# The gate products of a decoder trunk: two column tiles per call or four, on four accumulation banks

## The chip, the cores and the metric

The kernel runs on one core of one Trainium2 chip. The metric is the device time of one execution in microseconds (us); the figure given for a kernel is the median of its runs. One execution was also recorded by the hardware profiler, and the views of the profile come from that execution. In those views PE is TensorE's matrix multiplication, PEld its loading of the stationary operand, DVE is VectorE, ACT is ScalarE, POOL is GpSimd and SP is SyncE, which issues most of the DMA transfers. L253 means line 253 of the kernel that the view belongs to.

## The reference

Two layers of a post-norm decoder trunk, 256 tokens of width 1024, all in float32. Each layer is

```
x <- LN(alpha*x + 0.5*SwiGLU_1(x))
x <- LN(alpha*x + Mixer(x))
x <- LN(alpha*x + 0.5*SwiGLU_2(x))
```

with a feed-forward width of 2816. The change lies in the mixer:

```
z = x @ w_in                       # -> u | v | q | k | val | gate_A | gate_B, 1024 columns each
u, v = gelu(u), gelu(v)
h_a = u * chunked_causal_mix(LN(v))                      # branch A
q, k = rope(q), rope(k)                                  # 8 heads, 2 x 64
o = softmax(q1 k1^T) val - lam * softmax(q2 k2^T) val    # branch B, causal
h_b = rmsnorm(o) * (1 - lam_init)
m = sigmoid(gate_A) * (h_a @ W_A) + sigmoid(gate_B) * (h_b @ W_B)
Mixer(x) = m @ w_out
```

## The kernel before

**Numbers.** TensorE works on float32 values rounded to a shorter form (float32r). Each operand v is held as two parts, hi = v rounded and lo = v - hi, and a product is taken as hi*hi + lo*hi + hi*lo. The activations of a layer are kept as such pairs in `x_cat`: for each slab k of 128 of the 1024 inputs, 512 columns, of which the first 256 are the hi part of the 256 tokens and the last 256 their lo part. `both(k)` is that 512-column slab.

**Weights.** `stream` (L156 to L172) brings 1 MB of weights by one DMA from SP's queue into a buffer `raw` (four of them). ACT rounds it into `whi` (L169) and DVE subtracts into `wlo` (L171), each in two pieces of 128x1024, a piece being one column tile of 128 outputs with its eight slabs of inputs. There are eight buffers for hi pieces and eight for lo pieces. The order of TensorE's instructions is the order in which the program writes them; that of the other engines is set by a scheduler when the program is built, from priorities (`step()` raises them with every weight transfer) and from explicit orders (`behind(...)` places an instruction after a named one). Each engine runs its own queue in order.

**The products with outputs on the partitions, `gemm_a2`.** A call takes a list of sources of 1 MB, each two column tiles. For every tile it takes a bank and issues eight matmuls of 512 columns with `whi` as the stationary operand (L253): the bank's left half gets hi*hi, the right half hi*lo. When all the call's tiles have had this wide pass, each gets a narrow one: eight matmuls of 256 columns with `wlo` onto the left half (L260). Behind a tile's narrow pass ACT copies the right half to `r` (L261), and DVE adds the left half to it (L263, or L265 where there is a scale). The result, two tiles to a buffer of 512 columns, is called `gz` in the gates, `z` in the queries and keys, `bz` in the branch products; `r` and these are of a pool of three buffers in the gates.

**Banks.** PSUM has eight banks, in two rings of four. `bank()` gives out the main ring, in turn: a call of one source takes two main banks, a call of two sources all four. `side_bank()` gives the side ring, used by attention, transposes and the position mixing. A bank can be written again once both of its readers, ACT's copy and DVE's add, are done.

**Order of the mixer.** First `val`; then, for each of four pairs of heads, a call for the queries and one for the keys, each with its rotation in `rope`: two DMAs on SP's queue swap the rows (L601), DVE multiplies by the cosines (L604), POOL the swapped rows by the sines (L605), and DVE sums the two (L609). Then gate A in four calls of one source, gate B in four, `u` in two, the `v` products, `u` in two more, and the branch products, which use calls of two sources. Behind each gate call ACT takes two tanh (L735), one for each tile.

**Attention beside the products.** What attention needs is cut into steps that are placed between the tiles of the running products by a clock: each tile's wide pass counts 0.65 and each narrow pass 0.35 (`beat`), and a step is issued when its delay has run out. For one pair of heads the steps are: scores on TensorE (L629) with the row maxima on DVE (L641) and eight exponentials on ACT (L643); the combination of the two softmaxes on DVE (L652, behind a reciprocal at L660 and L661); a rearrangement by POOL (L184), a transposing DMA on SP's queue (L188), and four copies on ACT (L677); the product with the values on TensorE (L683, L685); its copy and its squares on ACT (L688, L693); a reciprocal root on POOL; four scalings on ACT (L702); and a second transposition with two roundings. The pairs start `4.5 + 2.1 * hp` counts after their keys, so the four pairs' steps are spread over the gate calls and the calls behind them.

Of the kernel before, what the change touches and what calls it, by code (L numbers as in the profile page):

```python
# [16 lines left out]
AF = mybir.ActivationFunctionType  # L17
# [5 lines left out]
T = 256  # L23
NT = T // P
KT = D // P
# [28 lines left out]
def trunk(ctx, tc, x, xT, w13a, w13b, w2, wb, wqk, wa, wbr, wo, gateb, sgug, sgub, sguwT, sgubias, lam, diffg,  # L54
          lng, lnb, lngT, lnbT, cosT, sinT, out):
    nc = tc.nc
    V, A, G, PE = nc.vector, nc.scalar, nc.gpsimd, nc.tensor
# [15 lines left out]
    def name(s):  # L73
        serial[0] += 1
        return f"{s}_{serial[0]}"

    def bank():
        return psum.tile([P, 512], F32, tag="main", name=name("bank"))

    def side_bank():  # L80
        return psum.tile([P, 512], F32, tag="side", name=name("sbank"))

    def slots(s, n, dtype=F32):

        return [act.tile([P, 512], dtype, tag="slot", name=name(s)) for _ in range((n + 1) // 2)]
# [11 lines left out]
    def t512(s, n=3):  # L97
        return tmp.tile([P, 512], F32, tag="main", name=name(s), bufs=n)

    def s512(s, n=4):  # L100
        return tmp.tile([P, 512], F32, tag="side", name=name(s), bufs=n)
# [21 lines left out]
    def beat(w):  # L123

        clock[0] += w
        for task in list(tasks):
            if task[0] <= clock[0]:
                turn(task)
# [21 lines left out]
    def stream(src, width=CH, sub=HC, lent=(), after=(None, None)):  # L150

        step()
        raw = raw_pool.tile([P, CH], F32, tag="raw", name=name("raw"))
        loaded[0] = nc.sync.dma_start(raw[:, :width], src).ins  # L156
        out = []
        for o in range(0, width, HC):
            if o // HC in lent:
                hi, lo = ([act.tile([P, 512], F32R, tag="slot", name=name(n)) for _ in range(2)] for n in ("lhi", "llo"))  # L160
                at = [(hi[j], lo[j]) for j in range(2)]
            else:
                hi = hi_pool.tile([P, HC], F32R, tag="hi", name=name("whi"))
                lo = lo_pool.tile([P, HC], F32R, tag="lo", name=name("wlo"))
                at = [(hi[:, p : p + sub], lo[:, p : p + sub]) for p in range(0, HC, sub)]
            for p, (h, w) in zip(range(0, HC, sub), at):
                r = raw[:, o + p : o + p + sub]
                with behind(latest[0]):
                    A.activation(h, r, AF.Copy)  # L169
                with behind(after[o // HC] or latest[1]):  # L170
                    V.tensor_tensor(out=w, in0=r, in1=h.bitcast(F32), op=ALU.subtract)  # L171
            out.append((hi, lo))  # L172
        return out
# [69 lines left out]
    def gemm_a2(srcs, xc, zs, rs=lambda: s512("r"), scale=1.0):  # L243

        b, got = [], []
        for src in srcs:
            got += stream(src)
            for hi, _ in got[-2:]:  # L250
                b.append(bank())
                for k in range(KT):
                    PE.matmul(b[-1], hi[:, k * P : (k + 1) * P], xc(k), start=k == 0, stop=False)  # L253
                beat(0.65)
        for n, (_, lo) in enumerate(got):
            s = slice(n % 2 * T, (n % 2 + 1) * T)
            if n % 2 == 0:
                r, z = rs(), zs(n // 2)
            for k in range(KT):
                PE.matmul(b[n][:, :T], lo[:, k * P : (k + 1) * P], xc(k)[:, :T], start=False, stop=k == KT - 1)  # L260
            emptied[0] = A.activation(r[:, s], b[n][:, T:], AF.Copy, scale=scale).ins  # L261
            if scale == 1.0:
                a = V.tensor_tensor(out=z[:, s], in0=b[n][:, :T], in1=r[:, s], op=ALU.add)  # L263
            else:
                a = V.scalar_tensor_tensor(out=z[:, s], in0=b[n][:, :T], scalar=scale, in1=r[:, s], op0=ALU.mult,  # L265
                                           op1=ALU.add)
            added[0] = a.ins
            beat(0.35)
            if n % 2:
                yield n // 2, z  # L270
# [95 lines left out]
    b = side_bank()  # L366
# [11 lines left out]
    gbh = const.tile([P, DEPTH, 2, KT], F32, name="gbh")  # L378
# [202 lines left out]
    def mixer(l, i, norm):  # L581
# [146 lines left out]
        for br, sec in ((0, GA_), (1, GB_)):  # L728
            gt = slots("gate", KT)
            gates.append(gt)  # L730
            for c in range(KT // 2):
                (_, b), = gemm_a2([wa[l, sec, c]], both, lambda m: t512("gz"), lambda: t512("r"))
                for n in range(2):
                    s = slice(n * T, (n + 1) * T)
                    A.activation(gt[c][:, s], b[:, s], AF.Tanh, scale=0.5,  # L735
                                 bias=gbh[:, l, br, c * 2 + n : c * 2 + n + 1])

        g_bc, b_bc = (bc_load(v[l], gates[0][0][:, :1]) for v in (sgug, sgub))
        us = []
# [30 lines left out]
        for h in range(2):  # L770
            s = slice(h * 512, h * 512 + 512)
# [57 lines left out]
    for l in range(DEPTH):  # L829
        norm = ffn(l, 0, 0, norm)  # L830
        norm = mixer(l, 1, norm)
        norm = ffn(l, 1, 2, norm, last=l == DEPTH - 1)
# [83 lines left out]
```

## Time and profile before

| | |
|---|---|
| median of three runs | 1220.29 us |
| the three runs | 1219.65, 1220.29 and 1221.74 us |
| the profiled execution | 1220.37 us |
| its span, first to last instruction | 1218.6 us |
| matmuls and weight loads | 6079 each |
| instructions of DVE, ACT, POOL | 1516, 1372, 392 |
| HBM read, written | 235.47 MB, 1.05 MB, together 194 GB/s over the span |
| granted TensorE clock | 9 of 9 tenths in every slice |

The span is what the profiler recorded between the first and the last instruction. In the page of the profile the busy time of an engine stands with its share of the span and, behind the x, its number of instructions. The chain is found from the last instruction backwards: at each step it goes to what released that instruction, or to the one before it on its engine, so its shares say which engine held the end. A row of the timeline gives start, duration, engine, line, operation, output and input, and, where the engine had been idle before it, that idle time with what ended it in brackets. `x2` there is two instructions, in one row; the duration then is of both.

### The profile page before, as it was taken

Reading aid. Unit: us, or ns where it says so; the run is one execution under the profiler, and the core shown is the slowest. Engines: PE = TensorE matmul, PEld = TensorE weight load, DVE = VectorE, ACT = ScalarE, POOL = GpSimd, SP = SyncE. Lnnn points to the kernel's source line nnn. Section 1 sums busy time; section 2 is a strip of 40 time slices with the busy share of each in tenths; the row PEclk is TensorE's granted clock in tenths of the full one; section 3 lists DMA queues with packets and bytes.
Section 4 is the critical chain, followed back from the end, with each engine's and each line's share of the span. In section 5 each row is a group of like instructions: output and inputs, shape, how many; then the busy total and the mean of one; then the engine's idle time right before and its main releaser. Section 6 shows DMA issues by size and latency. Waiting matters only on the chain.

```text
span 1218.6 us, 17027 instructions
## 1 busy us (share of the span) xinstructions
PE 1212.8 (100%) x6079; PEld 1025.6 (84%) x6079; DVE 887.9 (73%) x1516; ACT 716.0 (59%) x1372; POOL 283.1 (23%) x392
## 2 busy tenths in 40 slices
PE   9999999999999999999999999999999999999998
PEld 8888888888888888888888888888888888888887
DVE  6676667897688986766676756678875989676763
ACT  6465546669865555554455554466797664564740
POOL 1523100155320023230023330003544000323200
PEclk9999999999999999999999999999999999999999
DMA  9967645659564746867556757556675746667540
GB/s 343 328 196 240 242 173 178 242 192 274 194 214 144 250 157 211 246 203 259 190 164 204 250 194 259 205 183 221 215 206 189 250 155 226 189 224 243 178 185 35
DMA packets 103653, 257.55 MB, mean 211 GB/s; under 512 B 68320, under 2 KB 69392, under 8 KB 77456
## 3 DMA queue, kind: packets, MB, share of 16 engines
q1 hardware_dynamic: 99600, 243.82, 59.2%
q0 software_dynamic: 3536, 12.13, 3.3%
q8 instruction: 47, 0.77, 0.2%
q10 hardware_dynamic: 432, 0.52, 0.1%
q14 instruction: 38, 0.31, 0.1%
HBM read 235.47 MB, written 1.05 MB: 194 GB/s over the span
## 4 chain that ended last, share of the span: by engine, by line
PE 99%; DMA 0%; DVE 0%; ACT 0%; issue 0%; ACTq 0%
PE bank L241 64%; PE bank L253 19%; PE bank L260 10%; PE bank L356 2%; PE sbank L629 1%; PE sbank L507 1%; PE sbank L685 1%; PE sbank L786 1%; DMA xraw<-in_xT 0%; PE sbank L683 0%; PE sbank L479 0%; DVE xtok L487 0%; ACT whi L206 0%; DVE st L452 0%; DVE xtok L448 0%; ACT x L206 0%
## 5 line engine op out<-in xcount | busy, mean ns | idle before, releaser
L171 DVE TENSOR_TENSOR wlo<-raw,whi 128x512 fp32r<-128x512 f32 (+1 forms) x570 | 524.1, 954 | 133.1 <-ACT whi L169 87.7
L169 ACT ACTIVATE whi<-raw 128x512 fp32r<-128x512 f32 (+1 forms) x570 | 432.7, 799 | 234.3 <-PE bank L241 158.3
L241 PE MATMUL bank<-whi,x 128*128 128x512 f32 x1352 | 421.8, 390 | 0.0
L241 PEld LDWEIGHTS bank<-whi,x 128*128 128x128 f32 x1352 | 253.9, 188 | 52.6
L241 PE MATMUL bank<-wlo,x 128*128 128x512 f32 x676 | 263.1, 389 | 0.0
L253 PE MATMUL bank<-x,whi 128*128 128x512 f32 x768 | 183.9, 391 | 0.0
L253 PEld LDWEIGHTS bank<-x,whi 128*128 128x128 f32 x768 | 141.5, 188 | 28.1
L184 POOL COPY planes<-planes 128x512 uint16<-128x512 uint16 x80 | 83.3, 1068 | 321.2 <-DVE planes L539 321.2
L241 PEld LDWEIGHTS bank<-wlo,x 128*128 128x128 f32 x676 | 127.0, 188 | 25.7
L241 PE MATMUL bank<-whi,hhi 128*128 128x512 f32 (+1 forms) x374 | 141.2, 378 | 0.0
L241 PE MATMUL bank<-wlo,hhi 128*128 128x512 f32 (+1 forms) x374 | 141.0, 377 | 0.0
L241 PE MATMUL bank<-whi,hlo 128*128 128x512 f32 (+1 forms) x374 | 140.8, 377 | 0.0
L260 PEld LDWEIGHTS bank<-x,wlo 128*128 128x128 f32 x768 | 97.9, 191 | 3.6
L260 PE MATMUL bank<-x,wlo 128*128 128x256 f32 x768 | 100.4, 284 | 0.0
L192 POOL COPY planes<-planes 128x512 uint16<-128x512 uint16 x80 | 70.5, 925 | 91.7 <-DMA planes<-planes 91.4
L539 DVE TENSOR_TENSOR planes<-planes,bank 128x512 f32<-128x512 f32 x40 | 27.3, 683 | 86.4 <-issue 70.8
L538 ACT ACTIVATE planes<-bank 128x512 f32<-128x512 f32 x40 | 24.0, 599 | 102.8 <-PE bank L241 101.8
L605 POOL TENSOR_TENSOR swap<-swap,sin_t 128x512 f32<-128x512 f32 x16 | 29.5, 1843 | 235.0 <-DMA swap<-z 202.6
L241 PEld LDWEIGHTS bank<-whi,hlo 128*128 128x128 f32 x374 | 70.4, 188 | 13.1
L241 PEld LDWEIGHTS bank<-whi,hhi 128*128 128x128 f32 x374 | 70.4, 188 | 12.8
L241 PEld LDWEIGHTS bank<-wlo,hhi 128*128 128x128 f32 x374 | 70.4, 188 | 12.5
L261 ACT ACTIVATE r<-bank 128x256 f32<-128x256 f32 x128 | 46.5, 372 | 25.6 <-PE bank L260 25.6
(179 smaller groups left out, 1288.2 us busy)
## 6 DMA issues: line engine op xcount, KB each, us to landing
raw<-in_w13b SPq DMA_DIRECT2D x76, 1024.0 KB, 5.4
raw<-in_w SPq DMA_DIRECT2D x40, 1024.0 KB, 6.0
raw<-in_wa SPq DMA_DIRECT2D x24, 1024.0 KB, 5.1
raw<-in_wb SPq DMA_DIRECT2D x16, 1024.0 KB, 5.0
raw<-in_wqk SPq DMA_DIRECT2D x16, 1024.0 KB, 4.8
raw<-in_wbr SPq DMA_DIRECT2D x16, 1024.0 KB, 5.0
raw<-in_w13a SPq DMA_DIRECT2D x8, 1024.0 KB, 5.1
raw<-in_wo SPq DMA_DIRECT2D x8, 1024.0 KB, 4.9
```

The costliest lines, as they stand in the source:

```text
L169: A.activation(h, r, AF.Copy)
L171: V.tensor_tensor(out=w, in0=r, in1=h.bitcast(F32), op=ALU.subtract)
L184: G.tensor_copy(out=planes(out)[:, w], in_=numbers(src)[:, w])
L192: eng.tensor_copy(out=numbers(out)[:, w], in_=planes(src)[:, w])
L241: PE.matmul(ps, xx, w, start=start and n == 0, stop=stop and n == 2)
L253: PE.matmul(b[-1], hi[:, k * P : (k + 1) * P], xc(k), start=k == 0, stop=False)
L260: PE.matmul(b[n][:, :T], lo[:, k * P : (k + 1) * P], xc(k)[:, :T], start=False, stop=k == KT - 1)
L261: emptied[0] = A.activation(r[:, s], b[n][:, T:], AF.Copy, scale=scale).ins
L356: PE.matmul(ps[t][m], x[:, j, o + t * P : o + (t + 1) * P], y, start=k0 + j == 0 and o == 0 and y is hi, stop=k0 + j == KT - 1 and y is lo)
L538: silu[0] = A.activation(s, ps[0], AF.Silu).ins
L539: added[0] = V.tensor_tensor(out=s, in0=s, in1=ps[1], op=ALU.mult).ins
L605: turned_by[0] = G.tensor_tensor(out=s3, in0=s3, in1=s, op=ALU.mult).ins
```

## The change

The loops over gate calls go two sources at a time. Before, each of the four calls of a gate took one source of two column tiles: two wide passes, two narrow ones. Now each of two calls takes two sources: four wide passes, then four narrow ones. It holds for both gates, in both layers: 16 calls become eight. The number and shapes of the matmuls, the weights' transfers, the copies, the adds and the tanh are the same. The counts of `beat` are the same in sum, but a wide pass counts 0.65 and a narrow one 0.35, so the attention steps fall at other places among the passes. `gemm_a2` itself is as before.

```diff
@@ -728,12 +728,13 @@
         for br, sec in ((0, GA_), (1, GB_)):
             gt = slots("gate", KT)
             gates.append(gt)
-            for c in range(KT // 2):
-                (_, b), = gemm_a2([wa[l, sec, c]], both, lambda m: t512("gz"), lambda: t512("r"))
-                for n in range(2):
-                    s = slice(n * T, (n + 1) * T)
-                    A.activation(gt[c][:, s], b[:, s], AF.Tanh, scale=0.5,
-                                 bias=gbh[:, l, br, c * 2 + n : c * 2 + n + 1])
+            for c0 in range(0, KT // 2, 2):
+                for m, b in gemm_a2([wa[l, sec, c0 + m] for m in range(2)], both, lambda m: t512("gz"),
+                                    lambda: t512("r")):
+                    for n in range(2):
+                        s, c = slice(n * T, (n + 1) * T), c0 + m
+                        A.activation(gt[c][:, s], b[:, s], AF.Tanh, scale=0.5,
+                                     bias=gbh[:, l, br, c * 2 + n : c * 2 + n + 1])
 
         g_bc, b_bc = (bc_load(v[l], gates[0][0][:, :1]) for v in (sgug, sgub))
```

Line numbers below this place are one higher in the kernel after.

## The prediction

> **What bounds the kernel now.** I read the page first (busy shares, then the chain that ended last), then the chain row by row through the gates of layer 0, then the windows and the timelines of ACT, DVE and POOL there.
>
> ```profile
> span 1218.6 us, 17027 instructions
> PE 1212.8 (100%) x6079; PEld 1025.6 (84%) x6079; DVE 887.9 (73%) x1516; ACT 716.0 (59%) x1372; POOL 283.1 (23%) x392
> PE 99%; DMA 0%; DVE 0%; ACT 0%; issue 0%; ACTq 0%
> ```
>
> The end is set by TensorE alone: 99% of the chain is PE, and no other engine holds more than a trace of it. So a faster ACT or DVE is worth nothing, and the change can only gain by making PE's own sequence shorter, or lose by making PE wait. The chain through the gates, as start, length, what (us):
>
> ```profile
> 220.59 3.65 PE bank L253 x16
> 224.24 1.91 PE bank L260 x16
> 226.16 3.65 PE bank L253 x16
> ...
> 257.45 3.65 PE bank L253 x16
> 261.11 1.91 PE bank L260 x16
> ...
> 267.63 0.22 PE sbank L683 x2
> ...
> 268.97 0.95 PE bank L260 x8
> 269.92 3.65 PE bank L253 x16
> 273.57 1.70 PE sbank L629 x15
> 275.28 2.10 PE bank L260 x16
> ...
> 293.50 1.51 PE sbank L629 x16
> 295.01 2.11 PE bank L260 x16
> ```
>
> L253 is the w_hi pass (two tiles of eight matmuls at 512 columns), L260 the w_lo pass, L629 the attention scores, L683 with L685 the product of probabilities and values. The rows abut: PE waits for nobody in the gates. The first gate call starts at 257.45, and a pair of tiles takes 5.57 (220.59 to 226.16). Scores cost 1.51 and make the pass behind them 0.2 longer, so 1.7; the value product takes 1.34 (267.63 to 268.97).
>
> What stands close behind PE there is ACT. One window, with busy time of each engine:
>
> ```profile
> 261.00:306.00 45.00, 45.00 (x281) 39.54 (x280) 36.26 (x90) 42.51 (x115) 25.33 (x48) 1.00 0.75 223
> ```
>
> The fourth busy figure is ACT: 42.51 of 45 us, against 59% over the span. It converts the weights (L169), copies the banks out (L261), does the gates' tanh, and the exponentials and scalings of attention. The clock is 1.00.
>
> **What the change removes.** PE's instructions stay the same in number and shape. Eight of sixteen changes from wide to narrow passes go. What such a change costs is seen in the branch products, which are already done four tiles at a time (whole chain, later in layer 0):
>
> ```profile
> 392.61 7.28 PE bank L253 x32
> 399.89 3.83 PE bank L260 x32
> 403.72 17.71 PE bank L241 x78
> ```
>
> Four tiles take 11.11 there, against 2 x 5.57 = 11.14: 0.03 saved per merged call, 8 calls (4 in each of 2 layers): 0.24 us, bounds 0 and 0.5. The narrow matmuls keep their pace: 3.83/32 is 120 ns, as is 1.91/16. The Trainium skill, page "TensorE: Matmul & The Clock Gate", section "LDWEIGHTS (loading the stationary operand)", gives a load as its columns over 1.2, about 107 ns here, as long as a narrow matmul streams; by it, as an estimate, twice as many narrow matmuls in a row could leave the loads uncovered. The rows just compared say they don't.
>
> **What it takes away from the cover.** There are four main banks. Until now a call used two, and the next call's w_hi went to the other two: a bank had a whole call, over 5 us, to be copied and added out. Now a call fills all four, and the next one begins on the first of them. After its last w_lo matmul the first bank has three w_lo passes, 3 x 0.96 = 2.9 us, before PE wants it again; each later bank has 0.87 more (1.83 for the w_hi tile in between, less 0.96). Draining is ACT's copy r, then DVE's add (gz), both queued in order behind whatever the built program has put there. I walk it in layer 0 by the order of the built program. ACT rows:
>
> ```profile
> 260.32 0.36 ACT L261 ACTIVATE r<-bank 128x256 f32<-128x256 f32 x1
> ...
> 261.89 2.00 ACT L169 ACTIVATE whi<-raw 128x1024 fp32r<-128x1024 f32 x2
> 263.79 0.37 ACT L261 ACTIVATE r<-bank 128x256 f32<-128x256 f32 x1
> 264.05 1.41 ACT L677 ACTIVATE aT<-d 128x512 uint16<-128x512 uint16 x2
> 265.32 0.81 ACT L677 ACTIVATE d<-d 128x256 uint16<-128x256 uint16 x2
> 265.99 0.35 ACT L261 ACTIVATE r<-bank 128x256 f32<-128x256 f32 x1
> 267.24 0.51 ACT L735 ACTIVATE gate<-gz,gbh 128x256 f32<-128x256 f32 x1 [0.89 <-DVE gz L263]
> ...
> 295.12 0.50 ACT L643 ACTIVATE pp<-pp,mx 128x256 f32<-128x256 f32 x1
> ...
> 298.64 0.63 ACT L261 ACTIVATE r<-bank 128x256 f32<-128x256 f32 x2
> 299.17 1.27 ACT L702 ACTIVATE on<-on,nwy 128x128 f32<-128x128 f32 x4
> ...
> 312.71 0.57 ACT L688 ACTIVATE on<-sbank 128x512 f32<-128x512 f32 x1
> 313.32 0.26 ACT L693 ACTIVATE sbank<-sbank 128x128 f32<-128x128 f32 x1
> ```
>
> and DVE rows:
>
> ```profile
> 260.71 0.42 DVE L263 TENSOR_TENSOR z<-bank,r 128x256 f32<-128x256 f32 x1 [0.94 <-ACT r L261]
> ...
> 281.29 0.17 DVE L660 RECIPROCAL rc<-sums 128x4 f32<-128x4 f32 x1
> 281.50 0.22 DVE L661 SCALAR_TENSOR_TENSOR c<-rc,neg_lam,sums 128x4 f32<-128x4 f32 x1
> 281.75 1.41 DVE L652 SCALAR_TENSOR_TENSOR d<-pp,c,pp 128x256 f32<-128x256 f32 x4
> ...
> 296.82 2.35 DVE L171 TENSOR_TENSOR wlo<-raw,whi 128x1024 fp32r<-128x1024 f32 x2
> 299.10 0.41 DVE L263 TENSOR_TENSOR gz<-bank,r 128x256 f32<-128x256 f32 x1
> ```
>
> Occupancy per piece, row start to row start: a conversion 0.95, r 0.27, four L677 1.94, the eight exponentials 295.12 to 298.64 = 3.52, four L702 1.2, a tanh about 0.41, L688 0.6, an L693 about 0.41 (0.26 and its readout).
>
> *First call, third tile.* It takes the bank of the last key tile, whose add ends at 260.71 + 0.42 = 261.13; PE wants it at 257.45 + 3.65 = 261.10. Wait 0.1 (0 to 0.25 with the hand-over).
>
> *PE without waits.* Call 1 with its value product ends at 269.92, as now. Call 2 has scores behind its second tile, from 273.57 as now, and ends at 273.57 + 1.7 + 3.65 + 3.83 = 282.8. Call 3 (gate B): three w_hi tiles 5.5, value product 1.34, w_hi 1.83, first w_lo 0.96, scores 1.7, three w_lo 2.9: 297.0. Call 4's second w_hi tile is wanted at 298.8, and needs call 3's second bank drained.
>
> *ACT and DVE.* Call 2's exponentials start 1.62 after the scores (293.50 to 295.12 now) and end at 275.2 + 3.52 = 278.7. DVE then needs 1.9 (281.29 to 283.16 now) for the probabilities, 1.2 for a w_lo and 0.4 for the add: 282.2. There ACT's tanh can start, and from it on ACT is never free: two tanh 0.8, r 0.27, L677 1.94, r 0.27, L702 1.2, two tanh and three conversions 3.7, L688 0.6, four L693 1.65, a conversion 0.95: 11.4, so 293.6 for the copy of call 3's first bank, which PE finished at 292.4. Copy, add and tanh: 295.0. Now eight exponentials stand ahead of the second bank's copy: 298.5, copied at 298.9; DVE's two w_lo (2.3, behind eight row maxima of 2.2 from 294.5) end at 299.05, its add at 299.45. PE waits 0.65. That is the low bound but for luck, since no hand-over and no stretched DVE row is in it. Some eight hand-overs of 0.03 to 0.1 and three w_lo stretched by 0.2 (POOL beside, below) make 1.65 the high one. I take 1.1.
>
> Covered at nothing: the temporaries (r and gz share three buffers; the next call comes 11 us later), the tanh, and the weight supply (223 GB/s in the window; the same transfers as now, conversions of two calls ahead). If that prefetch ran dry, a call's four tiles would want 2 MB in 7.3 us, 0.27 MB/us; then PE would wait on conversions.
>
> **One more wait moved.** In the built program DVE's sum of the last key tile (L609) now stands ahead of the first gate add, not behind it, and it waits for POOL's product:
>
> ```profile
> 237.87 1.29 POOL L605 TENSOR_TENSOR swap<-swap,sin_t 128x512 f32<-128x512 f32 x1 [5.75 <-DVE mx L641]
> 265.08 2.94 POOL L605 TENSOR_TENSOR swap<-swap,sin_t 128x512 f32<-128x512 f32 x1 [4.15 <-DMA swap<-z]
> 268.05 1.07 DVE L609 TENSOR_TENSOR qk<-qk,swap 128x512 f32<-128x512 f32 x1 [0.85 <-POOL swap L605]
> ```
>
> If the sum still starts at 268.05, then sum 1.0, w_lo 1.2 and add 0.4 end at 270.65, and call 2, due at 269.92, waits 0.7. But the product's 2.94 was spent beside a busy DVE; with DVE idle it may take 1.29 and the wait is 0. The Trainium skill, page "SBUF — State Buffer", section "Who interferes with whom", says that a DVE instruction with two SBUF inputs contends with a GpSimd instruction that reads SBUF; the two POOL rows agree, and by that rule the wait would be nearer 0. I take 0.2.
>
> **The sum.** Per layer 0.1 + 1.1 + 0.2 = 1.4, twice 2.8, less 0.24: +2.55. The profiled execution took 1220.37 (span 1218.6 and 1.8 around it), 0.08 over the median of 1220.29. That gives 1222.9.
>
> **Rivals.** *Drained in time (not slower).* If call 3's second add ends by 298.8, 0.65 sooner than I sum, the wait vanishes; it decides at that point, and ACT has idle time upstream (0.89 in the tanh row) to win it from. Then only 0.24 is saved: 1220.1. Against it: ACT's 11.4 us without a gap. *The sum on POOL (slower still).* L609 holds the queue the full 0.7 and the attention stretch runs late behind it, with the bank wait at 1.65: 2 x (0.25 + 0.7 + 1.65) - 0.24 = +5.0, 1225.4. *It changes nothing in PE's order* is excluded: the built program has four w_hi tiles, then four w_lo. *The bank rule.* The Trainium skill, page "Trainium Kernel Development and Optimization", section "Best Practices", warns of PSUM pressure and that regular bubbles can mean PSUM ran out; no bubble shows now, and the forecast is such a bubble.
>
> **How the numbers follow.** A change under 0.2% (2.4 us) can't be told from none: the three runs spread 2.1 us. Forecast case 0.56, its range 1221.3 to 1224.3, 0.36 of it over the bound; drained in time 0.18, split 0.17 same and 0.01 faster; POOL 0.20, slower; the rest 0.06, most of it an unseen gain, 0.05. Slower 0.56, same 0.38, faster 0.06. Range 1220.0 to 1225.8.
>
> **What would show it.** In the profile after, a gap of about 1 us in PE ahead of the second w_hi tile of gate B's second call in each layer, released by DVE's gz, with exponentials ahead of that copy on ACT; a four-tile call at 11.11. Wrong, if the gates' rows abut as now, or if PE waits on w_hi.

## The result, and the profile after

The kernel after takes 1223.60 us (median of ten runs, 1223.18 to 1224.48), the kernel before 1220.32 (ten runs beside them, 1219.65 to 1221.74). The ratio is 1.0029, with a 95% interval of 1.0020 to 1.0037: slower by 3.28 us. The prediction said 1222.9, 1220.0 to 1225.8.

The page of the profile after: its span, the busy time of the engines, and the shares of the chain that ended last.

```profile
span 1221.6 us, 17009 instructions
PE 1213.7 (99%) x6079; PEld 1025.3 (84%) x6079; DVE 887.4 (73%) x1516; ACT 716.6 (59%) x1372; POOL 277.8 (23%) x392
PE 93%; ACT 4%; POOL 1%; DVE 1%; issue 1%; DMA 0%; ACTq 0%
```

TensorE does as many matmuls as before, but the chain no longer runs on it alone: 4% lie on ACT, which had 0%. The span is 3.0 longer. The list of waits says what TensorE waited for (us in total, times, longest); before it had no row for the gates.

```profile
PE bank L253 <- DVE gz L263: 2.0, 4, 0.7
```

Four waits of the wide pass for a gate's add, two in each layer. Where they are, and what they cost, is read from the timeline of TensorE, before and then after. What stands in brackets is the idle time. It is less than the delay, since the recorded matmuls overlap (256.92 + 7.66 is later than the next start, 264.42), so delays are taken from start to start: eight wide matmuls take 1.82 (the 3.65 of sixteen, halved), 32 wide 7.28, 32 narrow 3.83.

```profile
257.29 3.82 PE L253 MATMUL bank<-x,whi 128*128 128x512 f32 x16
...
308.09 2.00 PE L253 MATMUL bank<-x,whi 128*128 128x512 f32 x8
```

```profile
256.92 7.66 PE L253 MATMUL bank<-x,whi 128*128 128x512 f32 x32
264.42 4.00 PE L260 MATMUL bank<-x,wlo 128*128 128x256 f32 x32
...
296.70 2.00 PE L253 MATMUL bank<-x,whi 128*128 128x512 f32 x8
298.97 5.78 PE L253 MATMUL bank<-x,whi 128*128 128x512 f32 x24 [0.27 <-DVE gz L263]
304.58 3.99 PE L260 MATMUL bank<-x,wlo 128*128 128x256 f32 x32
309.27 2.11 PE L253 MATMUL bank<-x,whi 128*128 128x512 f32 x8 [0.70 <-DVE gz L263]
```

Call the stretch from gate A's first matmul to `u`'s first "the stretch". In layer 0 it is 308.09 - 257.29 = 50.80 before and 309.27 - 256.92 = 52.35 after; in layer 1, read in the same way, 50.64 and 52.37. The two differences make 1.55 + 1.73 = 3.28, which is the loss within its interval (2.4 to 4.5 us); that it meets the difference of the medians to the last digit is chance. (Where only one stretch is given below, it is that of layer 0.) In layer 0 TensorE is late at three places:
- gate A's first call, third tile: 264.42 - 256.92 = 7.50, so 0.22 late
- gate B's second call, second tile: 304.58 - 296.70 = 7.88, so 0.60 late
- `u`'s first call, first tile: 309.27 - 304.58 = 4.69, so 0.86 late; this is no gate call, but it begins on the first bank that gate B's second call used.

The three make 1.68; in layer 1, read in the same way, they are 0.23, 0.56 and 0.90, so 1.69. Against the differences of the stretches that leaves -0.13 and +0.04 for all the rest: the saved changes of pass, and the scores, which take 1.60 for 1.71 in layer 0 and 1.62 for 1.54 in layer 1. A gain of 0.12 a layer can't be read out of that.

The second of them on ACT and DVE after:

```profile
294.54 0.49 ACT L643 ACTIVATE pp<-pp,mx 128x256 f32<-128x256 f32 x1
...
298.06 0.90 ACT L261 ACTIVATE r<-bank 128x256 f32<-128x256 f32 x3
300.44 0.70 ACT L702 ACTIVATE on<-on,nwy 128x128 f32<-128x128 f32 x2 [1.49 <-POOL nwy L234]
...
304.77 1.03 ACT L169 ACTIVATE whi<-raw 128x1024 fp32r<-128x1024 f32 x1
305.71 0.89 ACT L717 ACTIVATE hb<-onT,dgs 128x256 fp32r<-128x256 f32 x2
306.51 1.99 ACT L169 ACTIVATE whi<-raw 128x1024 fp32r<-128x1024 f32 x2
308.40 0.36 ACT L261 ACTIVATE r<-bank 128x256 f32<-128x256 f32 x1
```

```profile
260.19 0.41 DVE L263 TENSOR_TENSOR z<-bank,r 128x256 f32<-128x256 f32 x1
...
266.35 1.07 DVE L609 TENSOR_TENSOR qk<-qk,swap 128x512 f32<-128x512 f32 x1 [1.20 <-POOL swap L605]
...
296.23 2.36 DVE L171 TENSOR_TENSOR wlo<-raw,whi 128x1024 fp32r<-128x1024 f32 x2
298.50 0.41 DVE L263 TENSOR_TENSOR gz<-bank,r 128x256 f32<-128x256 f32 x1
...
308.80 0.42 DVE L263 TENSOR_TENSOR gz<-bank,r 128x256 f32<-128x256 f32 x1 [0.54 <-ACT r L261]
```

Eight exponentials (294.54 to 298.06) stand between the copies of gate B's first call's first and second bank; the second copy is at 298.06 and its add ends at 298.91, 0.06 ahead of TensorE's restart. Then the third place: TensorE finished the first bank of gate B's second call at about 305.54 (304.58 plus a quarter of 3.83), but ACT copies it at 308.40, and the add ends at 309.22. Ahead of the copy stand three weight conversions and two roundings for attention, none of which TensorE needs in the next 10 us: the conversions are for the `v` products, two calls ahead, whose first matmul is at 321.87, and the roundings for the branch products behind them. ACT had also sat idle for 1.49 before that, waiting for POOL's reciprocal root (300.44).

### The profile page after: what moved, and what is told of

Read it like the earlier page. It is cut to its first block, busy times and chain, and to the rows that moved or that the text cites. A ratio compares the mean times of both kernels' runs of the same rounds, so it can differ in the third digit from the quotient of the medians.

```text
span 1221.6 us, 17009 instructions
## 1 busy us (share of the span) xinstructions
PE 1213.7 (99%) x6079; PEld 1025.3 (84%) x6079; DVE 887.4 (73%) x1516; ACT 716.6 (59%) x1372; POOL 277.8 (23%) x392
## 4 chain that ended last, share of the span: by engine, by line
PE 93%; ACT 4%; POOL 1%; DVE 1%; issue 1%; DMA 0%; ACTq 0%
PE bank L241 64%; PE bank L253 16%; PE bank L260 8%; PE bank L356 2%; ACT whi L169 1%; PE sbank L507 1%; ACT gate L736 1%; PE sbank L787 1%; ACT pp L643 1%; PE sbank L629 0%; ACT sbank L693 0%; PE sbank L685 0%; ACT aT L677 0%; ACT on L702 0%; DMA xraw<-in_xT 0%
## 5 line engine op out<-in xcount | busy, mean ns | idle before, releaser
L605 POOL TENSOR_TENSOR swap<-swap,sin_t 128x512 f32<-128x512 f32 x16 | 26.8, 1676 | 234.9 <-DMA swap<-z 203.8
```

The lines of the kernel that those rows point to most:

```text
L605: turned_by[0] = G.tensor_tensor(out=s3, in0=s3, in1=s, op=ALU.mult).ins
```

## The experiments

All kept the matmuls' number and shapes; all but the first two and the last also kept the order of the kernel that they edit. Each time stands beside the kernel before on the same chip: 1220.09 for the first four, 1220.30 for the last four. Profiled executions differ by up to 2.3 us in what lies ahead of the gates, so the stretch is compared, not the span.

**Gate A alone, gate B alone.** The edit, `br == 0` in the one and `br == 1` in the other:

```diff
-            for c0 in range(0, KT // 2, 2):
-                for m, b in gemm_a2([wa[l, sec, c0 + m] for m in range(2)], ...
+            per = 2 if br == 0 else 1
+            for c0 in range(0, KT // 2, per):
+                for m, b in gemm_a2([wa[l, sec, c0 + m] for m in range(per)], ...
```

> Gate A in calls of two sources, gate B in calls of one as before. Theory (banks: the loss is TensorE waiting for main banks to be drained, at three places in each layer: gate A's first call, third tile, 0.2 us; gate B's second call, second tile, 0.55; u's first call, first tile, 0.88): only the 0.2 is left, the stretch from gate A's first matmul to u's first is 51.0 us in layer 0 (50.8 before, 52.35 with both gates changed), and the time is 0.4 over before, 1220.7. Rival (a call of four tiles costs by itself, whichever gate): half of the loss, the stretch 51.6, the time 1221.9.

> Gate B in calls of two sources, gate A in calls of one as before. Theory (banks): the waits of 0.55 at gate B's second call and 0.88 at u's first call stay, the stretch is 52.1 to 52.2 us, the time 2.8 over before, 1223.1. Rival (a call of four tiles costs by itself): half of the loss, the stretch 51.6, the time 1221.9.

Gate A alone: 1220.53, ratio 1.0002 (0.9993 to 1.0011), stretch 50.97. Gate B alone: 1223.04, ratio 1.0026 (1.0016 to 1.0035), stretch 52.07. The timeline of TensorE with gate B alone:

```profile
296.70 2.00 PE L253 MATMUL bank<-x,whi 128*128 128x512 f32 x8
299.32 5.73 PE L253 MATMUL bank<-x,whi 128*128 128x512 f32 x24 [0.62 <-DVE gz L263]
304.89 3.99 PE L260 MATMUL bank<-x,wlo 128*128 128x256 f32 x32
309.32 2.14 PE L253 MATMUL bank<-x,whi 128*128 128x512 f32 x8 [0.43 <-DVE gz L263]
```

Both waits of gate B are there, a little differently shared out (304.89 - 296.70 = 8.19, 0.91 late; 309.32 - 304.89 = 4.43, 0.60 late). So the loss is not half and half. Four tiles per call cost gate A next to nothing, with the same passes on the same four banks; they cost gate B what is ahead of its copies.

**The drain first.** The gates' copies and adds get an earlier priority (`soon`), nothing else. In the diff below, `ahead` runs its argument inside `first()`, which is `soon` for the gates' calls and does nothing for all other calls.

```diff
-            emptied[0] = A.activation(r[:, s], b[n][:, T:], AF.Copy, scale=scale).ins
+            emptied[0] = ahead(lambda: A.activation(r[:, s], b[n][:, T:], AF.Copy, scale=scale)).ins
...
-                a = V.tensor_tensor(out=z[:, s], in0=b[n][:, :T], in1=r[:, s], op=ALU.add)
+                a = ahead(lambda: V.tensor_tensor(out=z[:, s], in0=b[n][:, :T], in1=r[:, s], op=ALU.add))
...
-                                    lambda: t512("r")):
+                                    lambda: t512("r"), first=soon):
```

> The change, with the gates' copies and adds given an earlier priority: on ACT the copy of gate B's first call's second bank goes ahead of four of the eight exponentials, on DVE its add ahead of one conversion. Matmuls and their order are the same. Theory (banks): the copy comes 1.5 us and the add 1.1 us sooner, the wait of 0.55 at gate B's second call goes; the wait at u's first call stays, 0.3 to 0.9, since nothing moves ahead of the weight conversions there. The stretch is 51.5 to 51.8 us, the time about 1222.4. Rival (a call of four tiles, or the attention steps' new places among the passes, cost by themselves): as with the change, 52.35 us and 1223.6.

1221.38, ratio 1.0013 (1.0004 to 1.0022); stretch 51.17. ACT, DVE and TensorE in its timeline:

```profile
296.49 0.36 ACT L261 ACTIVATE r<-bank 128x256 f32<-128x256 f32 x1
...
299.57 0.70 ACT L702 ACTIVATE on<-on,nwy 128x128 f32<-128x128 f32 x2 [0.25 <-POOL nwy L234]
...
307.12 0.36 ACT L261 ACTIVATE r<-bank 128x256 f32<-128x256 f32 x1
```

```profile
297.34 0.41 DVE L263 TENSOR_TENSOR gz<-bank,r 128x256 f32<-128x256 f32 x1
```

```profile
296.68 7.44 PE L253 MATMUL bank<-x,whi 128*128 128x512 f32 x32
303.96 3.99 PE L260 MATMUL bank<-x,wlo 128*128 128x256 f32 x32
308.09 2.11 PE L253 MATMUL bank<-x,whi 128*128 128x512 f32 x8
```

The second bank's copy comes at 296.49 instead of 298.06, its add at 297.34 instead of 298.50, and the 32 wide matmuls take 303.96 - 296.68 = 7.28: the wait is gone. The wait at `u` fell as well, to 308.09 - 303.96 - 3.83 = 0.30, the low end of what I had given, and the stretch came out 0.33 under my range. ACT's copy there comes 1.28 earlier (307.12 for 308.40): its first scaling behind POOL's reciprocal root starts 0.87 sooner (299.57 for 300.44), and a tanh that stood behind that scaling now stands ahead of it, so that ACT is idle for 0.25 where it was for 1.49.

**The conversions of `v` behind.** They are placed after gate B's last copy and add: `stream` places its conversions behind the two instructions that `latest` holds, ACT's behind the first and DVE's behind the second.

```diff
-        us = []
+        us, latest_ends = [], (emptied[0], added[0])
...
-        u_part((0, 1))
+        u_part((0, 1)); latest[:] = latest_ends
```

> The change, with the weight conversions of the v products (ACT and DVE) placed behind the last copy and add of gate B. Matmuls and their order are the same. Theory (banks): at u's first call the copy of gate B's second call's first bank no longer stands behind three conversions, the wait of 0.88 goes to 0.1 or less; the 0.55 stays. The stretch is 51.5 us, the time about 1221.8. Rival 1 (ACT is late there because it waited 1.49 us for POOL's reciprocal root): the copy is still late and 0.5 or more of the 0.88 stays, stretch 52.0. Rival 2 (the cost is of the call itself): 52.35 us and 1223.6.

1221.29, ratio 1.0010 (1.0001 to 1.0019); stretch 51.47. ACT and TensorE:

```profile
300.55 0.69 ACT L702 ACTIVATE on<-on,nwy 128x128 f32<-128x128 f32 x2 [1.49 <-POOL nwy L234]
...
305.88 0.39 ACT L261 ACTIVATE r<-bank 128x256 f32<-128x256 f32 x1
```

```profile
299.08 5.76 PE L253 MATMUL bank<-x,whi 128*128 128x512 f32 x24 [0.27 <-DVE gz L263]
304.67 4.00 PE L260 MATMUL bank<-x,wlo 128*128 128x256 f32 x32
308.50 2.00 PE L253 MATMUL bank<-x,whi 128*128 128x512 f32 x8
```

308.50 - 304.67 = 3.83: the wait at `u` is gone, and the one at gate B's second tile stays, as expected. ACT waited just as long for POOL as with the change (1.49), so that wait alone does not make the copy late (rival 1 falls): it takes the conversions on top of it. The run before shows the other half: with the conversions in place and ACT idle for only 0.25, 0.30 of the wait was left.

**Both edits**, on the change and on the kernel before.

> The change with both edits: the gates' copies and adds earlier, and the v products' conversions behind gate B's last copy and add. Theory (banks): the waits at gate B's second call (0.55) and at u's first call (0.88) are both gone, only the 0.2 of gate A's first call is left. From the run with the first edit alone (51.18, of which 0.4 at u's first call) the stretch should be 50.8 us, as before the change; the time 1220.2. Rival (ACT and DVE have too much to do in this stretch, so that a wait taken away comes back elsewhere): 51.2 or more, 1221.2.

> The kernel before (two tiles per call) with the same two edits as both_fixed. Theory (banks): TensorE waits for nobody in the gates there, so the edits have nothing to take away: the stretch stays 50.8 and 50.6 us in the two layers, the time 1220.1. Rival (the edits help by themselves, whatever the size of a call): the time 1 us or more under before.

On the change: 1220.50, ratio 1.0003 (0.9994 to 1.0011), stretch 50.94. On the kernel before: 1219.66, ratio 0.9996 (0.9987 to 1.0004), stretch 50.68. The chain with both edits on the change:

```profile
299.09 7.28 PE bank L253 x32
306.37 3.83 PE bank L260 x32
310.20 1.84 PE bank L253 x8
```

Both came out near what I had given. The rows of gate B's second call abut again: 7.28, 3.83, then `u`. In the two stretches 0.61 of the 3.28 is left (0.14 and 0.47), about what the wait at gate A's third tile makes: that pass takes 7.53 in layer 0 and 7.72 in layer 1, where 7.28 is free of it. On the kernel before the edits bring nothing that can be told, since there was no wait.

**The third wait too.** On top of the other two edits, DVE's conversions for gate A's second call are put behind the adds of the last key tile.

```diff
             for c0 in range(0, KT // 2, 2):
+                latest[1] = key_add if c0 else latest[1]
```

> The same, and DVE's conversions for gate A's second call are placed behind the adds of the last key tile, so that the add for which gate A's third tile waits has one conversion less ahead of it. Theory (banks): the last 0.2 goes too, no wait in TensorE's gates, the stretch is 50.6 us, and the time 1219.8, which is no change against before that could be told: four tiles per call save nothing by themselves. Rival (four tiles per call are a gain that the waits hid): the stretch 50.2 or less, the time 1219.2. Rival 2 (the conversions that are moved come late for gate A's second call): a wait for ACT or DVE at its narrow passes, stretch over 51.

1224.18, ratio 1.0032 (1.0021 to 1.0044), stretch 53.29. The timeline of TensorE:

```profile
256.84 7.44 PE L253 MATMUL bank<-x,whi 128*128 128x512 f32 x32
264.12 4.00 PE L260 MATMUL bank<-x,wlo 128*128 128x256 f32 x32
...
270.58 3.92 PE L253 MATMUL bank<-x,whi 128*128 128x512 f32 x16 [1.12 <-DVE gz L263]
```

and of DVE:

```profile
268.97 1.21 DVE L171 TENSOR_TENSOR wlo<-raw,whi 128x1024 fp32r<-128x1024 f32 x1
270.11 0.41 DVE L263 TENSOR_TENSOR gz<-bank,r 128x256 f32<-128x256 f32 x1
```

A miss. The wait it aimed at is gone (264.12 - 256.84 = 7.28), but the conversions that I moved now stand ahead of gate A's first add on DVE: between the last key tile's add and this one there are four where there were two. The add comes at 270.11 instead of 268.89, and gate A's second call waits for it, 1.12 by the idle time; scores then wait 0.87 more. It was not the conversions alone: four L652 instructions ahead of two of them took 2.85 where they took 1.41 with the change. I had looked for a late conversion at the narrow passes; it was once more a late drain.

**Scores later.** The last head pair's attention starts 1.1 counts later.

```diff
-            beside(attend(hp, qT, kT), 4.5 + 2.1 * hp)
+            beside(attend(hp, qT, kT), 4.5 + 2.1 * hp + 1.1 * (hp == 3))
```

> The change, with the last head pair's attention started 1.1 counts later, so that its scores and exponentials stand behind gate B's first call's four narrow passes and no longer between the first and the second. No priorities are changed. Theory (exponentials ahead of the second bank's copy): the wait of 0.55 goes to 0, all four copies being done before the exponentials; these now run in front of the copies of gate B's second call, so the wait at u's first call stays or grows, 0.9 to 2.0. The stretch is 51.8 to 52.9 us, the time 1222.5 to 1224.5. Rival (the wait at the second tile does not hang on the exponentials, DVE's conversions are late by themselves): 0.4 or more of the 0.55 stays.

1236.65, ratio 1.0129 (1.0113 to 1.0144), stretch 54.11, where I had given 1222.5 to 1224.5 and 51.8 to 52.9:

```profile
296.84 7.55 PE L253 MATMUL bank<-x,whi 128*128 128x512 f32 x32
304.23 3.99 PE L260 MATMUL bank<-x,wlo 128*128 128x256 f32 x32
311.21 2.55 PE L253 MATMUL bank<-x,whi 128*128 128x512 f32 x8 [2.99 <-DVE gz L263]
```

At the second tile there is no wait (7.39 from start to start, of which 0.11 belongs to the scores ahead: behind them sixteen wide matmuls took 3.76 with the change, 274.96 to 278.72, where 3.65 is usual): with the exponentials behind the copies it goes, without any priority. The wait at `u` grew to 311.21 - 304.23 - 3.83 = 3.15, which is beyond the 2.0 that I gave. The exponentials stand ahead of that copy now, but so does an idle wait of ACT for POOL's root, 3.43 us at 299.25, so this run does not say what the exponentials alone cost there. The branch products wait for a late `hb` besides. By the idle times, the waits at `u` make 6.0 in the two layers and those for `hb` 5.2; with some 5 us lost to a halved clock (last section) that is about the 16.35 by which the run is slower.

## Why the prediction was right

- **What bounds the kernel**: right. The loss is TensorE's own waiting: the three delays make 1.68 and 1.69 in the two layers, 3.37 against 3.28 in the medians.
- **Little is won by fewer changes of pass** (predicted 0.12 a layer). Free of waits, a call of four tiles takes 7.28 + 3.83 = 11.11 (gate B's second call with both edits, in the chain above), against 2 x 5.57 = 11.14. The term is 0.03 a call, as in the forecast, too small for any run to show in the time. The narrow matmuls kept their 120 ns, 32 in a row, as read from the branch products; the estimate from the Trainium skill, page "TensorE: Matmul & The Clock Gate", section "LDWEIGHTS (loading the stationary operand)", that loads could come out uncovered is not borne out here.
- **Gate A's third tile** (0.1, at most 0.25): 0.22, at the place and for the reason given. The bank is that of the first of the two tiles in the last call for keys. Its add ended at 260.60 and TensorE wanted the bank at 260.57, so 0.03 late as in the forecast; the other 0.19 came behind the add.
- **The sum of the last key tile** (0.2; 0 to 0.7): 0. The sum started at 266.35, not at 268.05, and gate A's second call started without a wait. POOL's product started 0.58 sooner (264.50 for 265.08), and it took 1.82 and not 2.94, with DVE idle for 1.20 while it waited: "nearer 0", as the rule of the Trainium skill, page "SBUF — State Buffer", section "Who interferes with whom", had it, and here the trace agrees with it in direction. How much is not shown: the row of 1.29 that I read as one with DVE idle (237.87) stands beside a busy DVE, row maxima until 238.4 and then a conversion, which itself took 1.90 instead of 1.2.
- **Gate B's second tile** (1.1; 0.65 to 1.65): the mechanism was right, down to the exponentials ahead of the copy, and the size was off: 0.60, under even the low bound. The walk through ACT's queue was close: its tanh started at 282.14 (I had 282.2), the copy of the first bank at 293.26 (293.6), the exponentials at 294.54 (295.0), the copy of the second bank at 298.06 (298.5). The add ended at 298.91 (I had 299.45 without and 300.45 with all delays), and TensorE wanted the bank at 298.52 (I had 298.8), so the add was 0.39 late and not 0.65; the other 0.21 came behind the add, 0.06 until TensorE restarted and the rest in its first matmuls. What I had added for hand-overs and stretched rows did not happen: two conversions took 2.36, as before. That the pieces, taken from row start to row start, already held the hand-overs is my reading; no run tests it.
- **`u`'s first tile** (not in the sum): 0.86 in layer 0. This is the step that failed. I walked the drains up to gate B's second call and stopped there, since the edit stops there; but the banks that this call filled are the next call's, whoever makes it, and ACT had three conversions and two roundings in front of the copy, behind an idle wait of 1.49 for POOL that the forecast did not have either. The wait was 0.30 where ACT's copy came 1.28 sooner with the conversions in place, and none with the conversions behind the copy.

So the total, 2.55 forecast and 3.28 measured, is near for partly the wrong reason: the two over-sized terms (0.5 and 0.2 a layer) hide most of the one left out. That the time fell near the middle of the range is in part luck.

The Trainium skill's warning that regular bubbles can mean that PSUM ran out (page "Trainium Kernel Development and Optimization", section "Best Practices") is what came about: the same two gaps in both layers. But the banks did not have to become more: with both edits the same four banks and the same four tiles per call wait 0.25 in layer 0 and 0.44 in layer 1.

**What stays open.** Whether the change could come out ahead of the kernel before with all three waits gone was not run: the one attempt at the third made another wait. The calls free of waits leave little room for it, 0.03 each, 0.24 in all, which could not be told from none. No version here beat the kernel before by more than can be told; its two edits without the change stand at 0.9996, with 1 in the interval.

## What to carry to other kernels

When a call fills every bank of a ring, the engines that drain it come under TensorE's clock: count, for each bank and also for the next user of the ring, what stands in the queue ahead of its copy and add, because those queues run in order. Work that nobody needs soon (weight conversions two calls ahead, exponentials) belongs behind the drain, but look at which drain it then stands in front of: in the runs with the third wait and with later scores the moved work made a longer wait elsewhere. A larger batch has to save something to pay for this: here the passes already abutted, and there was next to nothing to save.

## What the runs showed of the hardware

A long wait costs more than itself. After the 2.99 us without matmuls in the run with later scores, the granted clock (the column behind POOL's) was full until 312 and then fell to half. Windows of 1 us:

```profile
312.00:313.00 1.00, 1.00 (x5) 0.85 (x4) 1.00 (x3) 1.00 (x5) 0.00 (x0) 0.84 0.41 90
313.00:314.00 1.00, 1.00 (x5) 0.81 (x5) 1.00 (x2) 0.54 (x2) 0.00 (x0) 0.50 0.78 131
...
316.00:317.00 1.00, 1.00 (x6) 0.87 (x6) 0.00 (x0) 0.65 (x2) 0.00 (x0) 0.95 0.88 262
```

That is some 3.4 us at half clock (312.7 to 316.1), about 1.7 lost, beginning 1.5 us after TensorE had started again; it is part of why that run lost more than its waits. The Trainium skill, page "TensorE: Matmul & The Clock Gate", section "HAM oscillation — how this bites in real kernels", puts the gap that does this at more than about 3.4 us; here 2.99 by the idle time, 3.15 by the delay, was enough. The run had three more long waits. Those with idle times of 2.78 (to 364.01) and 3.01 (to 923.85) were followed by 3.4 us at half clock as well, which began at about the restart and not 1.5 behind it; the one of 2.45 (to 976.18) was not. Where TensorE ran in these three stretches, half the time was lost, about 4.9 us. The waits of the change itself, 0.7 at the longest by the idle time, and the 1.12 in the run with the third wait lowered nothing.
